# Feed-forward with seven half-block products instead of eight, for 38 of 44 pairs of units

## The chip, the cores and the metric

The kernel runs on one core of a Trainium2 chip. The metric is the device time of one execution in microseconds; lower is better. A core has five engines that run side by side, each with its own list of instructions in a fixed order: TensorE (PE, matrix products; PEld are its weight loads), VectorE (DVE), ScalarE (ACT), GpSimd (POOL) and SyncE (SP, which issues most transfers). They wait for each other through semaphores.

## The reference

Two blocks are computed, one after the other. The change lies in the second one's feed-forward, which stands at the end of each of its two layers (here cut to what matters):

```
D_MODEL = 1024; FF_HIDDEN = 2816; 512 tokens, 256 context tokens
def swiglu(h, w_i, w_o):
    g, u = jnp.split(h @ w_i, 2, axis=-1)
    return (jax.nn.silu(g) * u) @ w_o
...
xl = xl + ml[5] * rms_norm(swiglu(adaln(xl, g[2], ml[3], ml[4]), w_ffn_in[l], w_ffn_out[l]), g[3])
if with_ctx:      # layer 0 only
    xc = xc + mc[5] * rms_norm(swiglu(adaln(xc, g[2], mc[3], mc[4]), w_ffn_in[l], w_ffn_out[l]), g[3])
```

`h @ w_i` has 2 x 2816 columns: 22 blocks of 128 for the gate g and 22 for u. Block m of g and block m of u make a pair of units; there are 22 pairs a layer and 44 in all.

## The kernel before, in words

All products are in float32 split in two: a value is hi + lo, where hi is the value rounded to a shorter form (fp32r) and lo is the rest, and a product is hi·hi + hi·lo + lo·hi, three matmuls. Weights come in by `wsplit` (L272): SP loads 128x1024 float32 values into a buffer `raw` (two buffers), ScalarE makes `hi` (L288), VectorE makes `lo` as raw - hi (L289); `hi` and `lo` have four buffers each. In a unit's raw tile the 1024 columns are 8 blocks of 128x128, one for each 128 of the 1024 inputs. The hidden activations lie transposed, as hTh and hTl (hi and lo), 8 blocks of 128 inputs by 512 tokens, and as hThc and hTlc for the 256 context tokens.

The pairs are worked through in chunks: pairs 0-1, 2-5, 6-9, 10-13, 14-17, then 18-19 and 20-21 in layer 0, 18-21 in layer 1. For each chunk `hidden` (L1672) makes each pair's product with the first weights: for each of its two units, 24 matmuls of 512 columns (`mm_a_g`, L301, L302, L305), in layer 0 also 24 of 256 columns for the context. Then come tanh on ScalarE (L1691), two products on VectorE (L1692, L1693) and the split of the result into `ph` (ScalarE) and `pl` (VectorE), both by `split_into` (L564). After the chunk's pairs, `part` (L1779) multiplies ph and pl by the second weights: for each block of 128 tokens (four in layer 1, six in layer 0) and each half of the 1024 outputs, three matmuls of 512 columns for each pair (`mm_b_g`, L321 to L323), which VectorE adds to `y` (L1791). The first chunk of a layer starts while the tokens are still being normalized, in halves of 256 tokens.

The order on each engine is that of the code, with two exceptions: weights are loaded and split early, by a priority of 3000 steps, as far as buffers allow, and in layer 0 a background (`mod_steps`, L433) of products for the modulation weights runs on VectorE, advanced by `tick`, which counts the columns that PE has been given. SP issues the loads in the order in which they are asked for; a load that waits for its buffer holds up the ones behind it.

Of the kernel before, what the change touches and what calls it, by code (L numbers as in the profile page):

```python
# [251 lines left out]
class Builder:  # L252
# [1418 lines left out]

    def hidden(self, l, ms, segs, fp, NN, bufs, late=None, post=None):  # L1672

        nc, A = self.nc, self.A
# [20 lines left out]
        return ph, pl  # L1695

    def layer2(self, l, hx, vx, hp, hT, hc, vt, fill, src, srcc, stop=None):
# [8 lines left out]
        hy = ExitStack()  # L1706
        hp = self.pool(hy, f"hy{l}")
        with tc.tile_pool(name=f"psf{l}", bufs=2, space=PSUM, reuse_waits="tile") as pp, ExitStack() as c1:
# [48 lines left out]
            ends = [0, 2, 6, 10, 14, 18, 20, 22] if l == 0 else [0, 2, 6, 10, 14, 18, 22]  # L1757
            chunks = [list(range(a, b)) for a, b in zip(ends, ends[1:])]
            ys = {}
            vt = fill = None  # L1760
            for ci, ch in enumerate(chunks):
# [7 lines left out]
                if ci:  # L1769
                    self.hf_act = last  # L1770
                for ms in [ch] if ci == 0 else [[m] for m in ch]:
                    h, lo = self.hidden(l, ms, ctxs + halves if ci == 0 else [(hT, 0, 0, T)] + ctxs, fp, 128 * nt,
                                        2 if last and l == 0 else 6, late if ci == 0 else None, post)
                    ph.update(h)
                    pl.update(lo)
# [17 lines left out]
                if not last:  # L1793
                    for n in range(2):
                        for c in order:
                            part(c, n)
                    if ci == len(chunks) - 2:
                        self.pump(100)
                    continue
                pend = []  # L1800
                for i, c in enumerate(order):
                    v = c // 4
                    ss, d = self.t(self.small, [128, 2], F32, "ss2", 7), []
                    for n in range(2):
                        part(c, n)
                        d.append(self.res_half(rp, ys[c][:, 512 * n:512 * n + 512], G[v], n, ss, n == 0))
# [146 lines left out]
```

## Time and profile before

| | us |
|---|---|
| median of three runs (2586.1 to 2595.94) | 2591.81 |
| the profiled execution | 2587.33 |
| its span in the profile | 2585.5 |
| PE busy in it | 2511.3 |
| VectorE (DVE) busy | 1516.8 |
| ScalarE (ACT) busy | 1031.9 |
| GpSimd (POOL) busy | 241.7 |

The mean granted clock of PE was 0.993 of 2.4 GHz. A row of a timeline gives the start, the duration, the engine, the line of the kernel, the operation with what it writes and reads, and in brackets how long the engine stood idle before it and what ended the wait. A matmul's duration is longer than its share of PE, since matmuls overlap; what one costs is read from the starts.

### The profile page before, as it was taken

How to read it: one execution, taken by the hardware profiler on the slowest of the kernel's cores; microseconds unless marked ns; L12 is line 12 of the kernel's file. 1: busy time of each engine (PE TensorE's matmuls, PEld its weight loads, DVE VectorE, ACT ScalarE, POOL GpSimd, SP SyncE). 2: the span in 40 equal slices, each digit the busy share in tenths (PEclk: the TensorE clock that was granted, in tenths of full speed). 3: DMA queues.
4: the chain of work that ended last, by engine and by line, in shares of the span. 5: the costliest groups of instructions: out<-in, count | busy, mean ns of one | idle time of the engine just before them, and what ended most of it. 6: DMA issues, size and time to landing. Idle time of an engine off the chain costs nothing.

```text
span 2585.5 us, 38643 instructions
## 1 busy us (share of the span) xinstructions
PE 2511.3 (97%) x15587; PEld 2071.2 (80%) x15587; DVE 1516.8 (59%) x2502; ACT 1031.9 (40%) x1962; POOL 241.7 (9%) x288
## 2 busy tenths in 40 slices
PE   8999999999999999999999999999999999999997
PEld 7777887787777888777988888888788777887886
DVE  5657588645365577666756544445567766443434
ACT  6523333333444544465631211212655466522222
POOL 0000012102000000512100000000100412000001
PEclk9999999999999999999999999999999999999999
DMA  5424364342131211522543333332211434322222
GB/s 187 159 73 162 107 228 131 98 131 74 58 130 66 82 34 53 146 81 101 190 146 123 131 122 105 127 120 90 90 58 50 120 110 147 115 91 97 91 97 81
DMA packets 85169, 284.63 MB, mean 110 GB/s; under 512 B 12176, under 2 KB 15072, under 8 KB 84608
## 3 DMA queue, kind: packets, MB, share of 16 engines
q1 hardware_dynamic: 78880, 263.50, 30.0%
q0 software_dynamic: 4864, 15.74, 2.2%
q10 hardware_dynamic: 1248, 2.95, 0.4%
q8 instruction: 122, 2.00, 0.3%
q14 instruction: 55, 0.45, 0.1%
HBM read 253.78 MB, written 21.00 MB: 106 GB/s over the span
## 4 chain that ended last, share of the span: by engine, by line
PE 77%; DVE 7%; issue 5%; ACT 5%; DMA 3%; POOL 2%; SPq 0%; DVEq 0%; POOLq 0%; ACTq 0%
PE acc L301 13%; PE acc L305 13%; PE acc L302 13%; PE acc L321 9%; PE acc L323 9%; PE acc L322 9%; DVE lo L289 2%; ACT hi L288 1%; PE tp L1460 1%; PE at L1431 1%; DMA raw<-in_wo 1%; PE tp L1453 1%; ACT junk L344 1%; ACT hf L388 1%; PE at L650 1%
## 5 line engine op out<-in xcount | busy, mean ns | idle before, releaser
L289 DVE TENSOR_TENSOR lo<-raw,hi 128x1024 fp32r<-128x1024 f32 (+1 forms) x321 | 388.0, 1211 | 400.0 <-ACT hi L288 279.2
L288 ACT ACTIVATE hi<-raw 128x1024 fp32r<-128x1024 f32 (+1 forms) x321 | 335.9, 1048 | 559.2 <-PE acc L323 228.4
L301 PE MATMUL acc<-hTh,hi 128*128 128x512 f32 (+1 forms) x1408 | 547.6, 393 | 5.2 <-ACT hTh L565 2.7
L302 PE MATMUL acc<-hTl,hi 128*128 128x512 f32 (+1 forms) x1408 | 542.2, 389 | 0.3 <-DVE hTl L566 0.2
L305 PE MATMUL acc<-hTh,lo 128*128 128x512 f32 (+1 forms) x1408 | 352.0, 388 | 0.0
L321 PE MATMUL acc<-hi,hTh 128*128 128x512 f32 (+3 forms) x832 | 317.0, 383 | 5.9 <-ACT hi L288 2.4
L301 PEld LDWEIGHTS acc<-hTh,hi 128*128 128x128 f32 x1408 | 266.7, 190 | 65.3 <-issue 3.9
L322 PE MATMUL acc<-lo,hTh 128*128 128x512 f32 (+3 forms) x832 | 310.9, 374 | 2.9 <-DVE lo L289 2.6
L323 PE MATMUL acc<-hi,hTl 128*128 128x512 f32 (+3 forms) x832 | 311.2, 375 | 0.4 <-DVE hTl L566 0.4
L302 PEld LDWEIGHTS acc<-hTl,hi 128*128 128x128 f32 x1408 | 267.4, 190 | 54.7 <-DVE hTl L566 0.7
L305 PEld LDWEIGHTS acc<-hTh,lo 128*128 128x128 f32 x1408 | 254.8, 188 | 55.8 <-issue 0.2
L321 PEld LDWEIGHTS acc<-hi,hTh 128*128 128x128 f32 x832 | 157.1, 189 | 38.4 <-issue 6.6
L322 PEld LDWEIGHTS acc<-lo,hTh 128*128 128x128 f32 x832 | 157.7, 190 | 29.4 <-DVE lo L289 7.1
L323 PEld LDWEIGHTS acc<-hi,hTl 128*128 128x128 f32 x832 | 157.4, 189 | 27.6 <-DVE hTl L566 2.7
L321 PE MATMUL acc<-hi,ph 128*128 128x512 f32 x440 | 175.0, 398 | 0.0
L323 PE MATMUL acc<-hi,pl 128*128 128x512 f32 x440 | 173.8, 396 | 0.0
L322 PE MATMUL acc<-lo,ph 128*128 128x512 f32 x440 | 173.3, 394 | 0.0
L301 PE MATMUL acc<-hThc,hi 128*128 128x256 f32 x608 | 149.2, 283 | 0.0
L302 PE MATMUL acc<-hTlc,hi 128*128 128x256 f32 x608 | 148.0, 281 | 0.0
L433 DVE SCALAR_TENSOR_TENSOR bgraw<-bgraw,cb 128x1024 f32<-128x1024 f32 x96 | 117.1, 1219 | 17.7 <-DMA bgraw<-in_w_mod 16.7
L1791 DVE TENSOR_TENSOR y<-y,acc 128x512 f32<-128x512 f32 x112 | 76.5, 686 | 82.1 <-PE acc L323 81.7
L301 PEld LDWEIGHTS acc<-hThc,hi 128*128 128x128 f32 x608 | 114.4, 188 | 2.5
(340 smaller groups left out, 3697.8 us busy)
## 6 DMA issues: line engine op xcount, KB each, us to landing
bgraw<-in_w_mod SPq DMA_DIRECT2D x96, 512.0 KB, 3.3
raw<-in_wf_in SPq DMA_DIRECT2D x88, 512.0 KB, 3.3
raw<-in_wf_out SPq DMA_DIRECT2D x44, 512.0 KB, 3.3
raw<-in_wb_a SPq DMA_DIRECT2D x38, 512.0 KB, 3.8
raw<-in_wi_a SPq DMA_DIRECT2D x36, 512.0 KB, 3.3
raw<-in_wo SPq DMA_DIRECT2D x32, 512.0 KB, 3.5
xt<-xd SPq DMA_DIRECT2D x16, 512.0 KB, 3.6
raw<-in_wb_v SPq DMA_DIRECT2D x12, 512.0 KB, 3.4
```

Of the source, the lines that this page charges most:

```text
L288: nc.scalar.activation(out=hi[:, :n], in_=raw[:, :n], func=AF.Copy)
L289: self.pin = nc.vector.tensor_tensor(out=lo[:, :n], in0=raw[:, :n], in1=hi[:, :n].bitcast(F32), op=ALU.subtract)
L301: mm(ps, lhsT=wh[:, k], rhs=xh[:, k, n0:n0 + n], start=(k == 0), stop=False)
L302: mm(ps, lhsT=wh[:, k], rhs=xl[:, k, n0:n0 + n], start=False, stop=False)
L305: mm(ps, lhsT=wl[:, k], rhs=xh[:, k, n0:n0 + n], start=False, stop=(k == KT - 1))
L321: mm(ps, lhsT=xh, rhs=wh[:, j], start=(k == 0), stop=False)
L322: mm(ps, lhsT=xh, rhs=wl[:, j], start=False, stop=False)
L323: mm(ps, lhsT=xl, rhs=wh[:, j], start=False, stop=(k == nk - 1))
L344: self.nc.scalar.activation(out=junk[:, :x.shape[-1]], in_=x, func=AF.Square, accum_out=dst)
L388: nc.scalar.activation(out=hf[:, j], in_=ps[:, j], func=AF.Identity, scale=a[:, k:k + 1], bias=b[:, k:k + 1])
L433: nc.vector.scalar_tensor_tensor(out, raw, 1.0, cb[:, v], ALU.mult, ALU.mult, accum_out=md[:, v, k:k + 1])
L1791: nc.vector.tensor_tensor(out=ys[c][:, hs], in0=ys[c][:, hs], in1=ps, op=ALU.add)
```

## The change

A pair's product is seen as a product of two matrices of 2 x 2 blocks: the weights A have the two units as rows and the two halves of the 1024 inputs as columns (A11 and A12 for the gate unit, A21 and A22 for the other), the activations B have the halves of the inputs as rows and the two halves of 256 tokens as columns. The plain product takes eight block products; the changed one takes seven, of sums of blocks:

- with token sums t1 = B12 - B11, t2 = B22 - t1, t3 = B22 - B12 and t4 = B21 - t2 (made once a layer, `token_sums`), and weight sums made for each pair from the raw weights;
- r1 = A11·B11, then + A12·B21 (the gate unit, first half of the tokens);
- r7 = A22·t4, then + (A11 - A21)·t3;
- r5 = (A21 + A22)·t1, then + (A12 - (A21 + A22 - A11))·B22;
- r2 = (A21 + A22 - A11)·t2;
- and the other three results by additions on VectorE, from s1 = A11·B11 + r2, s4 = A22·t4, s5 = (A21 + A22)·t1 - s4, r5 and r7.

Each block product is 12 matmuls of 256 columns (4 blocks of inputs, three matmuls each). The path is taken in both layers from the second chunk on, except in layer 0's last chunk: 18 and 20 pairs. The context's product in layer 0 stays as it was, with A22 and A21 of one unit and A11, A12 of the other. The sums of weights run on GpSimd, in place, on the raw tile; so a pair's raw weights are split four times (w[3], w[0], w[2], w[1]) instead of twice. The raw weights of these pairs go into other buffers: in layer 1 those of the first block's context activations, which are free by then and which the token sums also use as scratch. The first pair of a chunk has its weights prepared during the products with the second weights, and `part` leaves out its last pair's three matmuls until three parts have done the others. The diff, cut to its core:

```diff
+    def token_sums(self, hT, tt, xy):
+        ...
+        op(y, l[0][1], l[0][0], ALU.subtract, nc.gpsimd)
+        op(x, h[0][1], h[0][0], ALU.subtract)
+        op(x, x, y, ALU.add)
+        self.split_into(x, *tt[0])
+        op(y, h[1][1], x, ALU.subtract)
+        op(y, y, l[1][1], ALU.add)
+        self.split_into(y, *tt[1])
+        op(x, h[1][1], h[0][1], ALU.subtract, nc.gpsimd)
+        op(y, h[1][0], y, ALU.subtract)
+        op(y, y, l[1][0], ALU.add)
+        self.split_into(y, *tt[3])
+        op(x, x, l[1][1], ALU.add)
+        op(x, x, l[0][1], ALU.subtract)
+        self.split_into(x, *tt[2])
+
+    def sevens(self, l, hT, tt, hc, fp, rp, NN, raws, fa):
+        ...
+        def weights(m, early=False):
+            ...
+            w = ws[m] = {3: parts(pair(), rb, 512 if hc is None else 1024)}
+            op(a22, a21, a22, ALU.add)
+            op(a21, a11, a21, ALU.subtract)
+            yield
+            w2 = pair()
+            w[0] = parts(pair(), ra)
+            op(a11, a22, a11, ALU.subtract)
+            op(a12, a12, a11, ALU.subtract)
+            yield
+            w[2] = parts(w2, rb)
+            ...
+        def hidden(m, nxt, more):
+            ...
+            r7 = acc()
+            prod(r7, w[3], 1, t4, True)
+            ...
+            act(out=s4, in_=r7, func=AF.Copy)
+            ...
+            r1 = acc()
+            prod(r1, w[0], 0, b11, True)
+            act(out=s1, in_=r1, func=AF.Copy)
+            w[1] = parts(pair(), raw.pop(m)[0])
+            tail()
+            ...
+            r5 = acc()
+            prod(r5, w[2], 1, t1, True)
+            act(out=s5, in_=r5, func=AF.Copy)
+            tt2(s5, s5, s4, ALU.subtract)
+            next(nxt, 0)
+            prod(r7, w[2], 0, t3, False)
+            prod(r1, w[0], 1, b21, False)
+            next(nxt, 0)
+            more()
+            ...
+            gate(a[:, :256], r1)
+            r2 = acc()
+            prod(r2, w[1], 0, t2, True)
+            tt2(s1, s1, r2, ALU.add)
+            tt2(c21, s1, r7, ALU.add)
+            tt2(c22, c21, s5, ALU.add)
+            prod(r5, w[1], 1, b22, False)
+            next(nxt, 0)
+            ...
+                tt2(c12, s1, r5, ALU.add)
+                gate(a[:, 256:], c12)
+                yield from out(a, c2, ph[:, :T], pl[:, :T])
...
+            def raws(m):
+                if l == 0:
+                    pool, tag = ((fp, "raw"), (self.wraw, "raw"))[m % 2]
+                    return [self.t(pool, [128, 1024], F32, tag, 2) for _ in range(2)]
+                t = self.t(hp0, [128, 2, 1024], F32, ("hThc", "hTlc")[m % 2])
+                return t[:, 0], t[:, 1]
...
-                    self.mm_b(ps, lambda k: (ph[ch[k]][:, sl], pl[ch[k]][:, sl]), us[n], len(ch))
+                    g = self.mm_b_g(ps, lambda k: (ph[ch[k]][:, sl], pl[ch[k]][:, sl]), us[n], len(ch))
+                    for _ in range(len(ch) - 1):
+                        next(g)
+
+                    yield
+                    drain(g)
```

VectorE in layer 1, one pair within a chunk, before. The names are those of the code; fa is the gate's buffer, acc a product's result in PSUM, and the numbers tell tiles apart.

```order
L289 TENSOR_TENSOR lo_21542<-raw_21539,hi_21541 128x1024
L1692 SCALAR_TENSOR_TENSOR fa_21438<-fa_21438,acc_21413 128x512
L289 TENSOR_TENSOR lo_21548<-raw_21545,hi_21547 128x1024
L1693 SCALAR_TENSOR_TENSOR fa_21438<-fa_21438,acc_21441 128x512
L566 TENSOR_TENSOR pl_21400<-fa_21438,ph_21399 128x512
```

VectorE in layer 1, one pair within a chunk, now. dy and hf are the buffers of the copies s1, s4, s5 and of the sums; the raw weights lie in hThc and hTlc.

```order
L1737 TENSOR_TENSOR dy_23102<-dy_23102,dy_23101 128x256
L1746 TENSOR_TENSOR lo_23145<-hThc_23050,hi_23144 128x512
L1746 TENSOR_TENSOR lo_23177<-hThc_23050,hi_23176 128x1024
L1787 SCALAR_TENSOR_TENSOR fa_23185<-fa_23185,acc_23109 128x256
L1737 TENSOR_TENSOR dy_23101<-dy_23101,acc_23188 128x256
L1737 TENSOR_TENSOR hf_23103<-dy_23101,acc_23088 128x256
L1737 TENSOR_TENSOR hf_23103<-hf_23103,dy_23102 128x256
L1746 TENSOR_TENSOR lo_23175<-hThc_23050,hi_23174 128x1024
L1737 TENSOR_TENSOR dy_23102<-dy_23101,acc_23129 128x256
L1787 SCALAR_TENSOR_TENSOR fa_23185<-fa_23185,dy_23102 128x256
L1790 SCALAR_TENSOR_TENSOR fa_23185<-fa_23185,hf_23103 128x512
L1746 TENSOR_TENSOR lo_23256<-hThc_23050,hi_23255 128x1024
```

Five rows have become thirteen (the pair's last, the lo of its result, L1737 into pl, comes right behind the last row here): four splits of weights instead of two, and nine operations on results instead of three, four of which read PSUM (acc).

GpSimd at the same place, now; before, it has no row there between the last normalization of the tokens and the end of the layer. The rows are the two token sums of layer 1 and the weight sums of its first six pairs on the new path, four each.

```order
L1705 TENSOR_TENSOR hThc_21511<-hTl_20855 128x1024
L1705 TENSOR_TENSOR hThc_21511<-hTh_20854 128x1024
L1760 TENSOR_TENSOR hThc_21530<-hThc_21530 128x512 x4
L1760 TENSOR_TENSOR hTlc_21629<-hTlc_21629 128x512 x4
L1760 TENSOR_TENSOR hThc_21722<-hThc_21722 128x512 x4
L1760 TENSOR_TENSOR hTlc_21854<-hTlc_21854 128x512 x4
L1760 TENSOR_TENSOR hThc_21986<-hThc_21986 128x512 x4
L1760 TENSOR_TENSOR hTlc_22293<-hTlc_22293 128x512 x4
```

Each of these reads and writes SBUF alone.

VectorE at the start of the new path in layer 1, now: the token sums stand among the last operations of the first chunk (L566 into hTl are the last splits of the normalized tokens, L1692 to L1693 and L566 into pl the first chunk's results).

```order
L1705 TENSOR_TENSOR hThc_21511<-hThc_21511,hTl_20855 128x1024
L566 TENSOR_TENSOR pl_21210<-fa_21422,ph_21209 128x256
L1693 SCALAR_TENSOR_TENSOR fa_21478<-fa_21478,acc_21481 128x256
L566 TENSOR_TENSOR hTl_21510<-hThc_21511,hTh_21509 128x1024
L566 TENSOR_TENSOR pl_21224<-fa_21478,ph_21223 128x256
L1705 TENSOR_TENSOR hThc_21511<-hTh_20854,hThc_21511 128x1024
L1705 TENSOR_TENSOR hThc_21511<-hThc_21511,hTl_20855 128x1024 x2
L566 TENSOR_TENSOR hTl_21510<-hThc_21511,hTh_21509 128x1024 x2
L1746 TENSOR_TENSOR lo_21614<-hThc_21530,hi_21613 128x512
L1746 TENSOR_TENSOR lo_21622<-hThc_21530,hi_21621 128x1024
```

The last two rows are the first split weights of the third pair, whose raw tile (hThc_21530) is the same memory as the scratch of the token sums (hThc_21511).

## Rows read from the trace of the kernel before

**Rows 1.** The page: span, busy time of the engines, the chain.
```profile
span 2585.5 us, 38643 instructions
PE 2511.3 (97%) x15587; PEld 2071.2 (80%) x15587; DVE 1516.8 (59%) x2502; ACT 1031.9 (40%) x1962; POOL 241.7 (9%) x288
PE 77%; DVE 7%; issue 5%; ACT 5%; DMA 3%; POOL 2%; SPq 0%; DVEq 0%; POOLq 0%; ACTq 0%
```

**Rows 2.** Feed-forward stretches: length, PE, PEld, DVE, ACT, POOL busy, clock, DMA, GB/s.
```profile
1312.00:1790.00 478.00, 478.00 (x2498) 405.08 (x2497) 248.16 (x382) 99.53 (x138) 0.00 (x0) 1.00 0.36 120
2230.00:2555.00 325.00, 325.00 (x1388) 260.09 (x1387) 130.16 (x152) 88.23 (x104) 0.33 (x1) 1.00 0.27 91
```

**Rows 3.** Timeline of PE, layer 0: starts of products with 512, then 256 columns.
```profile
1426.95 0.39 PE L301 MATMUL acc<-hTh,hi 128*128 128x512 f32 x1
...
1432.57 0.39 PE L301 MATMUL acc<-hTh,hi 128*128 128x512 f32 x1
...
1438.19 0.28 PE L301 MATMUL acc<-hThc,hi 128*128 128x256 f32 x1
...
1441.01 0.28 PE L301 MATMUL acc<-hThc,hi 128*128 128x256 f32 x1
```

**Rows 4.** Groups by line and shape: busy us, mean ns | idle before.
```profile
L289 DVE TENSOR_TENSOR lo<-raw,hi 128x1024 fp32r<-128x1024 f32 x304 | 372.1, 1226 | 378.5 <-ACT hi L288 274.7 <-PE acc L305 94.0 <-issue 6.3
L433 DVE SCALAR_TENSOR_TENSOR bgraw<-bgraw,cb 128x1024 f32<-128x1024 f32 x96 | 117.1, 1219 | 17.7 <-DMA bgraw<-in_w_mod 16.7
L1791 DVE TENSOR_TENSOR y<-y,acc 128x512 f32<-128x512 f32 x112 | 76.5, 686 | 82.1 <-PE acc L323 81.7
L566 DVE TENSOR_TENSOR pl<-fa,ph 128x512 fp32r<-128x512 f32 x40 | 27.7, 693 | 28.0 <-ACT ph L565 28.0
L1692 DVE SCALAR_TENSOR_TENSOR fa<-fa,acc 128x512 f32<-128x512 f32 x40 | 27.4, 684 | 49.7 <-ACT fa L1691 49.7
L1692 DVE SCALAR_TENSOR_TENSOR fa<-fa,acc 128x256 f32<-128x256 f32 x30 | 12.4, 415 | 0.1
...
L288 ACT ACTIVATE hi<-raw 128x1024 fp32r<-128x1024 f32 x304 | 321.8, 1060 | 533.4 <-PE acc L323 228.2 <-PE acc L302 203.8 <-DMA raw<-in_wf_in 18.7
L565 ACT ACTIVATE ph<-fa 128x512 fp32r<-128x512 f32 x40 | 25.3, 632 | 157.3 <-DVE fa L1693 157.3
L1691 ACT ACTIVATE fa<-acc 128x256 f32<-128x256 f32 x30 | 11.2, 373 | 0.0
...
L1521 POOL TENSOR_TENSOR oh<-oh,gth 128x512 f32<-128x512 f32 x10 | 12.9, 1288 | 54.9 <-DVE gth L1520 54.8
...
L301 PEld LDWEIGHTS acc<-hThc,hi 128*128 128x128 f32 x608 | 114.4, 188 | 2.5
```

**Rows 5.** Timeline, GpSimd beside VectorE at three places: start us, us, instruction.
```profile
1218.01 2.54 POOL L1655 TENSOR_TENSOR vt<-vt,G 128x512 f32<-128x512 f32 x2
...
1219.58 2.06 DVE L289 TENSOR_TENSOR lo<-raw,hi 128x1024 fp32r<-128x1024 f32 x1 [2.08 <-ACT hi L288]
...
2168.99 1.23 DVE L289 TENSOR_TENSOR lo<-raw,hi 128x1024 fp32r<-128x1024 f32 x1 [0.54 <-ACT hi L288]
2169.64 1.72 POOL L1655 TENSOR_TENSOR vt<-vt,G 128x512 f32<-128x512 f32 x1 [0.61 <-ACT junk L344]
...
2554.67 1.30 POOL L1655 TENSOR_TENSOR y<-y,G 128x512 f32<-128x512 f32 x1 [348.27 <-ACT junk L344]
2555.02 0.69 DVE L1791 TENSOR_TENSOR y<-y,acc 128x512 f32<-128x512 f32 x1 [0.24 <-PE acc L323]
```

**Rows 6.** The page's DMA issues: count, KB each, us from issue to landing.
```profile
raw<-in_wf_in SPq DMA_DIRECT2D x88, 512.0 KB, 3.3
```

**Rows 7.** Stretches at the start of layer 1's feed-forward, columns as in rows 2.
```profile
2190.00:2196.00 6.00, 1.60 (x11) 0.99 (x9) 4.65 (x9) 5.95 (x14) 0.00 (x0) 1.00 0.72 249
2196.00:2200.00 4.00, 3.88 (x18) 3.69 (x19) 2.37 (x4) 3.81 (x9) 0.54 (x1) 0.57 0.44 137
2200.00:2204.00 4.00, 4.00 (x36) 4.00 (x35) 3.13 (x6) 2.11 (x6) 0.54 (x1) 1.00 0.65 227
```

More of the change, by code (lines that the diff above doesn't have):

```diff
@@ L1670, in norm_vecs, with hidden @@
         return a[:, v], b[:, v]
-    def hidden(self, l, ms, segs, fp, NN, bufs, late=None, post=None):
+    def hidden(self, l, ms, segs, fp, NN, bufs, fa, late=None, post=None):
         nc, A = self.nc, self.A
@@ L1695, in hidden, with op @@
         return ph, pl
+    def token_sums(self, hT, tt, xy):
+        nc = self.nc
+        h, l = [[[x[:, 4 * k:4 * k + 4, 256 * t:256 * t + 256].bitcast(F32) for t in range(2)] for k in range(2)] for x in hT]
+        x, y = xy
+        def op(o, a, b, op, e=nc.vector):
+            e.tensor_tensor(out=o, in0=a, in1=b, op=op)
+        op(y, l[0][1], l[0][0], ALU.subtract, nc.gpsimd)
[12 more added lines that the diff above has]
+        self.split_into(x, *tt[2])
@@ L1706, in layer2 @@
         hy = ExitStack()
-        hp = self.pool(hy, f"hy{l}")
+        hp0, hp = hp, self.pool(hy, f"hy{l}")
         with tc.tile_pool(name=f"psf{l}", bufs=2, space=PSUM, reuse_waits="tile") as pp, ExitStack() as c1:
@@ L1758, in layer2 @@
             chunks = [list(range(a, b)) for a, b in zip(ends, ends[1:])]
+            end7 = ends[-2] if l == 0 else ends[-1]
             ys = {}
@@ L1770, in layer2 @@
                     self.hf_act = last
[L1771 to L1775, printed above, removed]
+                seven = ci > 0 and not (last and l == 0)
+                if seven:
+                    for m in ch:
+                        ph[m], pl[m] = s7[2](m, s7[1](m + 1) if m + 1 in ch else iter(()),
+                                             lambda: s7[0](m + 2) if m + 1 in ch and m + 2 < end7 else None)
+                    s7[3]()
+                else:
+                    for ms in [ch] if ci == 0 else [[m] for m in ch]:
+                        h, lo = self.hidden(l, ms, ctxs + halves if ci == 0 else [(hT, 0, 0, T)] + ctxs, fp, 128 * nt,
+                                            2 if last and l == 0 else 4, 3 if last and l == 0 else fa, late if ci == 0 else None, post)
+                        ph.update(h)
+                        pl.update(lo)
+                if ci == 0:
+                    tt = sums()
+                    self.token_sums(hT, tt, [x.rearrange("p (k n) -> p k n", n=256) for x in raws(0)])
+                    s7 = self.sevens(l, hT, tt, hc, fp, rp, 128 * nt, raws, fa)
+                    s7[0](ch[-1] + 1)
                 us = [None, None]
@@ L1794, in layer2 @@
                     for n in range(2):
-                        for c in order:
-                            part(c, n)
+                        gs = [part(c, n) for c in order]
+                        for i in range(0, nt, 3):
+                            for _ in range(2):
+                                for g in gs[i:i + 3]:
+                                    next(g, 0)
+                    if ch[-1] + 1 < end7:
+                        with tc.high_priority(offset=3000):
+                            drain(s7[1](ch[-1] + 1, True))
+                        s7[0](ch[-1] + 2)
                     if ci == len(chunks) - 2:
@@ L1804, in layer2 @@
                     for n in range(2):
-                        part(c, n)
+                        drain(part(c, n))
                         d.append(self.res_half(rp, ys[c][:, 512 * n:512 * n + 512], G[v], n, ss, n == 0))
```

84 lines of the change are left out of this document (83 added, 1 removed).

## The prediction

> **What bounds the kernel now.** I read the page's busy shares and chain first. PE is busy 97% of a span of 2585.5 us, the chain lies on PE for 77% of it, and VectorE, at 59%, is the only other engine above 40% [rows 1]. Then the stretches: in most of layer 0's feed-forward (1312 to 1790 us) and of layer 1's (2230 to 2555 us) PE has no gap at all, its granted clock is 1.00, which is the 2.4 GHz level, and GpSimd does nothing [rows 2]. So an us of PE taken out there is an us of time, as long as the others keep up. VectorE is busy 52% of the first stretch and 40% of the second, with background products of the modulation weights in the first.
>
> **The gross saving.** In layer 0 a unit's product for the 512 tokens starts at 1426.95 and the next at 1432.57: 24 matmuls in 5.62 us, 0.234 each; 24 matmuls of 256 columns (the context's) take 2.82 us, 0.1175 each [rows 3]. So two matmuls of 256 columns cost one of 512 almost exactly. A pair was 48 x 0.234 = 11.24 us; the seven products are 7 x 12 = 84 matmuls of 256 columns, 84 x 0.1175 = 9.87 us. That is 1.37 us a pair and 52.1 us for 38 pairs (24.7 in layer 0, 27.4 in layer 1) if no one is late.
>
> A rule of the Trainium skill speaks against this term: by "TensorE: Matmul & The Clock Gate", section "Back-to-back issue gap", the spacing in a stream of weight loads and matmuls is set by both, about 81 ns at 128 columns and 131 ns at 512. A straight line between the two gives an estimate of 98 ns at 256, so 84 x 0.098 = 8.2 us against 48 x 0.131 = 6.3, and the seven would be 1.9 us a pair slower. The two spacings of [rows 3] disagree with it, and they decide.
>
> **What is added beside it, layer 1.** By the program's order a pair now has on VectorE four subtractions for lo (one of them half size, since without context only half of the fourth weight block is needed), seven 256-column operations, one product of 512 and the lo of the result; on GpSimd four sums of 128x512 of the raw weights, where it had none; on ScalarE four hi, three copies, two tanh and one ph. Nearest rows [rows 4]: lo 128x1024 1.226 us, VectorE 128x256 0.415, 128x512 0.684 and 0.693, GpSimd 128x512 1.288, ScalarE hi 1.060, 128x256 0.373, 128x512 0.632. VectorE: 3 x 1.226 + 0.693 + 7 x 0.415 + 0.684 + 0.693 = 8.65 us; ScalarE: under 3.9 + 5 x 0.373 + 0.632 = 6.4; GpSimd: 4 x 1.288 = 5.15. Each by itself is below 9.87, and the gain would stand.
>
> But they aren't by themselves. While GpSimd's L1655 runs from 1218.01 to 1220.55, the lo started at 1219.58 takes 2.06 us [rows 5]: against its mean of 1.226 it lost 0.83 us, and most of its work came after GpSimd's end. At 2169.64 it is the other way about: a lo is running and GpSimd's operation takes 1.72 instead of 1.29. A VectorE add of which one input is in PSUM (2555.02) starts inside a GpSimd operation and still takes 0.69. So operations with both inputs in SBUF and GpSimd's run one after the other. The Trainium skill says the same more sharply ("SBUF — State Buffer", section "Who interferes with whom"): the second read port is one exclusive lock, held for the whole instruction, and a VectorE instruction with two SBUF inputs contends. By it the engines' times add; without it the larger alone would count. The rows agree with the lock.
>
> Of the 8.65 us, four 256-column operations read PSUM; the rest, 6.99 us, is locked: 6.99 + 5.15 = 12.14 us a pair, more than the 9.87 of the products and more than the old 11.24. The lower bound of the pace is thus 9.87 (the lock seldom meets), the upper 12.14 for a pair whose preparation falls within the pair before. I take nearly the upper one, because both the rows and the written order set GpSimd's sums right beside the lo's. The first pair of a chunk has its weights prepared during the products with the second weights (8 x 12 x 0.234 = 22.5 us, in which VectorE has little to do): 9.9 us. The second starts with a little lead: 11.0. The third and fourth are paced: 12.1 each. Sum 45.1 against 4 x 11.24 = 44.96, and about 0.3 for the tail of a chunk. PE's waits will stand at the fifth and seventh products (the second weight block's hi and lo behind GpSimd's sums). Five chunks: -2 us in all, where 27.4 were gained gross. Layer 1's whole gain goes.
>
> **Layer 0.** Here a pair has the context's 48 matmuls as well, 5.64 us, so 15.5 us of PE. The fourth weight block is whole (+0.53) and the context's result adds a lo of 0.415 under the lock (and two operations from PSUM): 13.1 us, below 15.5. The gain stands in most pairs. What stands against it is the background (L433, two SBUF inputs, 1.219 us). In chunks 2-5 and 6-9 one pair each has four of them: 13.1 + 4 x 1.22 = 18.0, -2.5 us each. Behind chunk 2-5 the order sets 15 of them, 12 y adds (L1791's 0.686), four lo, three early lo and GpSimd's four sums into products of 12 x 12 x 0.234 = 33.7 us: 18.3 + 8.2 + 4.9 + 3.7 + 5.15 = 40.3, up to -6.6; I take -5, since the y adds read PSUM and go beside GpSimd. Tails -2.5. Layer 0: 24.7 - 5 - 5 - 2.5 = +12 us (bounds: +24.7, and +5).
>
> **The two entries.** The token sums are new work between the first chunk and the first seven-product pair: eight VectorE sums and four lo of 128x1024 (12 x 1.226 = 14.7 us), four hi, and two GpSimd sums of that size, which no row shows: 1.29 to 2.6 us (one or two of 128x512), I take 2.5. In layer 1 a VectorE sum stands ahead of the last hTl, behind GpSimd's first sum: PE waits some 2.7 us for hTl. The raw weights of the third pair (index 2) go into the buffer that the token sums use as scratch, so that their load starts only after the last lo. Landing takes 3.3 us [rows 6], hi of half size 0.6 and lo 0.69: 4.6 us behind the last token sum, which ends about when PE has run out of the first chunk's products (96 x 0.1175 + 48 x 0.234 = 22.5 us, against 14.7 + 2.5 + some 5 us of other VectorE work). Then GpSimd's two sums, hi and lo, 4.9 us, must be in before the fifth product, with 2.8 us of products ahead: another 2. And idling costs twice: after the waits at 2190 to 2196 the clock was at 0.57 for 4 us, 18 matmuls where the next 4 us hold 36 [rows 7], so 1.7 us go after such a stop. 2.7 + 4.6 + 2 + 1.7, less what overlaps: -10 in layer 1 (bounds -5, -13). In layer 0 the scratch is the same, but 768 tokens give half as much cover again: -4 (-1, -7). The last chunk of layer 1 drains its parts one by one, so that the last pair's tail (0.415 + 0.373 + 0.415 + 0.684 + 0.632 + 0.693 = 3.2 us) has 9 x 0.234 = 2.1 us of cover: -1.5 with what follows.
>
> The raw loads are as many as before and land within a pair's time. The loads of the second weights stand behind them on SP's queue and are asked for a chunk ahead: nothing.
>
> **Sum**, against the profiled execution: +12 - 4 - 2 - 10 - 1.5 = -5.5. Its time was 2587.3 (span 2585.5), so 2592.8; the median of the runs shown is 4.5 above it, and on that scale I say 2597.
>
> **Rivals.**
> *The saving comes through (16%).* GpSimd's sums fall beside the waits of VectorE and the lock costs little; both layers keep 1.37 a pair and only entries and ends count: 52.1 - 14 - 1.5 = 36.6, 2555. For it: VectorE idles half the time in rows 2. Against it: 12.14 against 9.87, in three pairs of four.
> *Half of it (17%).* Layer 0 keeps all its 24.7, since the context's products cover the lock and the background moves aside, layer 1 is neutral, and the entries cost 4 instead of 14: 24.7 - 2 - 4 - 1.5 = 17, 2575.
> *Slower (23%).* One mechanism: PE's waits in layer 1's paced pairs are each over 2 us (12.1 - 9.9), a good part of the 4.4 us (of 6) that PE stood idle before the clock fell [rows 7]. If every paced pair pays the 1.7 us of half clock, 15 x 1.7 = 25.5 us come on top: 2623. It decides if the waits come in one piece; split between the fifth and the seventh product, they may be too short.
> *Weight loads bind (2%).* A weight load lasts 0.19 us, longer than 0.1175; if the new stream couldn't hide it, 84 x 0.188 = 15.8 us a pair, 4.6 more, 2760 or so. The context's matmuls of [rows 3] have the same loads and don't show it.
>
> **Numbers.** The forecast itself has 42%, with its own range of 2583 to 2610. A measurement of this kernel tells 0.5%, 13 us, from no change: 2579 to 2605. Faster: 16 + 12 of the half case + 4 of the forecast's lower edge = 32%. Slower: 23 + 2 + 4 of its upper edge = 29%. Same: 39%. The range goes to 2553, leaving out half of the first rival, and up to 2627, leaving out the last and a third of the slower case.
>
> **What would show it.** Right: in layer 1 PE's waits at the new products name VectorE's lo and ScalarE's hi of the second weight block, VectorE's lo means well over 1.23 us, GpSimd's sums over 1.29, chunks of about 45 us; in layer 0 the pairs without background take 15.5 us, without waits; PE stands still for 8 to 11 us at layer 1's first seven-product pair. Wrong: PE has no gap in 2230 to 2555 (first rival), or its granted clock falls in every pair there (third), or 84 matmuls take other than 9.9 us.

## The result: slower by 0.7%

The changed kernel takes 2611.23 us (median of four runs, 2608.51 to 2614.53), the kernel before 2593.88 beside it. The ratio is 1.0072, with a 95% interval of 1.0045 to 1.0098. The forecast was 2597, with a range up to 2627 and its weight on "no change": the time lies in the range, just above the forecast's own part of it (2583 to 2610) and nearer to the rival called slower.

### The profile page after: what moved, and what is told of

It reads as the page before. It is cut to its first block, busy times and chain, and to the rows that moved or that the text cites. A ratio compares the mean times of both kernels' runs of the same rounds, so it can differ in the third digit from the quotient of the medians.

```text
span 2608.6 us, 42234 instructions
## 1 busy us (share of the span) xinstructions
PE 2490.1 (95%) x16955; PEld 2115.7 (81%) x16955; DVE 1738.5 (67%) x2830; ACT 1136.7 (44%) x2198; POOL 513.1 (20%) x444
## 5 line engine op out<-in xcount | busy, mean ns | idle before, releaser
L289 DVE TENSOR_TENSOR lo<-raw,hi 128x1024 fp32r<-128x1024 f32 (+2 forms) x245 | 295.0, 1207 | 231.4 <-ACT hi L288 176.6
L288 ACT ACTIVATE hi<-raw 128x1024 fp32r<-128x1024 f32 (+2 forms) x245 | 255.1, 1043 | 282.7 <-PE acc L302 113.9
L301 PE MATMUL acc<-hTh,hi 128*128 128x512 f32 (+1 forms) x800 | 307.1, 391 | 5.2 <-ACT hTh L565 2.7
L302 PE MATMUL acc<-hTl,hi 128*128 128x512 f32 (+1 forms) x800 | 301.4, 383 | 2.7 <-DVE hTl L566 2.6
L1776 PE MATMUL acc<-hTh,hi 128*128 128x256 f32 x776 | 195.9, 285 | 12.6 <-ACT hi L1736 6.4
L305 PE MATMUL acc<-hTh,lo 128*128 128x512 f32 (+1 forms) x800 | 197.3, 381 | 0.0
L1777 PE MATMUL acc<-hTl,hi 128*128 128x256 f32 x776 | 192.8, 281 | 0.0
L301 PEld LDWEIGHTS acc<-hTh,hi 128*128 128x128 f32 x800 | 153.0, 192 | 37.0 <-issue 3.2
L302 PEld LDWEIGHTS acc<-hTl,hi 128*128 128x128 f32 x800 | 153.1, 192 | 30.0 <-DVE hTl L566 3.5
L305 PEld LDWEIGHTS acc<-hTh,lo 128*128 128x128 f32 x800 | 140.1, 188 | 27.8 <-issue 0.2
L1776 PEld LDWEIGHTS acc<-hTh,hi 128*128 128x128 f32 x776 | 146.7, 189 | 18.4 <-ACT hi L1736 8.6
```

The source lines that it names most:

```text
L288: nc.scalar.activation(out=hi[:, :n], in_=raw[:, :n], func=AF.Copy)
L289: self.pin = nc.vector.tensor_tensor(out=lo[:, :n], in0=raw[:, :n], in1=hi[:, :n].bitcast(F32), op=ALU.subtract)
L301: mm(ps, lhsT=wh[:, k], rhs=xh[:, k, n0:n0 + n], start=(k == 0), stop=False)
L302: mm(ps, lhsT=wh[:, k], rhs=xl[:, k, n0:n0 + n], start=False, stop=False)
L305: mm(ps, lhsT=wl[:, k], rhs=xh[:, k, n0:n0 + n], start=False, stop=(k == KT - 1))
L1776: mm(ps, lhsT=wh[:, 4 * o + k], rhs=xh[:, k], start=(first and k == 0), stop=False, skip_group_check=True)
```

## The profile after

The page, as [rows 1]: PE is busy 21 us less in a span 23 us longer; VectorE has 222 us more, GpSimd twice its time.

```profile
span 2608.6 us, 42234 instructions
PE 2490.1 (95%) x16955; PEld 2115.7 (81%) x16955; DVE 1738.5 (67%) x2830; ACT 1136.7 (44%) x2198; POOL 513.1 (20%) x444
```

Four stretches, columns as in [rows 2]: layer 0's chunk 2-5, its chunk 10-13, layer 1's chunk 2-5 and its chunk 6-9, the matmuls of the first weights each time.

```profile
1318.00:1391.00 73.00, 66.90 (x529) 65.81 (x530) 62.12 (x90) 29.15 (x51) 30.48 (x16) 0.95 0.34 117
1531.00:1594.50 63.50, 62.88 (x532) 62.62 (x531) 47.67 (x69) 26.70 (x47) 19.39 (x12) 1.00 0.32 110
2256.00:2304.00 48.00, 44.05 (x338) 41.78 (x339) 33.46 (x48) 23.22 (x40) 28.25 (x16) 0.96 0.23 84
2327.00:2369.00 42.00, 40.81 (x334) 39.66 (x334) 31.18 (x46) 21.10 (x37) 21.33 (x12) 1.00 0.26 92
```

Where PE had no gap it now has some, and in the first chunk of each layer on the new path the clock falls too. Cut into stages by the starts on PE's timeline (first and second: the products with the first and second weights; us), the two traces stand so:

| stage | before | after | difference |
|---|---|---|---|
| up to layer 0's feed-forward | 1254.4 | 1258.6 | +4.2 |
| layer 0: chunk 0-1, first + second | 37.5 + 16.8 | 40.6 + 19.7 | +6.0 |
| layer 0: first of 2-5, 6-9, 10-13, 14-17, 18-19 | 67.8, 67.6, 67.8, 67.6, 33.8 | 72.2, 67.9, 63.3, 65.9, 31.3 | -4.0 |
| layer 0: their second | 33.6 x4, 16.9 | 35.0, 37.3, 34.7, 33.8, 18.7 | +8.2 |
| layer 0's feed-forward as a whole, last chunk included | 572.4 | 581.0 | +8.6 |
| between the feed-forwards | 369.2 | 372.3 | +3.1 |
| layer 1: chunk 0-1, first + second | 26.9 + 11.2 | 29.0 + 15.8 | +6.7 |
| layer 1: first of the five chunks | 45.0 x5 | 47.1, 42.5, 42.4, 42.5, 42.5 | -8.0 |
| layer 1: second of the first four | 22.5 x4 | 23.0, 23.6, 24.3, 24.8 | +5.6 |
| layer 1: the last second products and the end | 36.4 | 39.3 | +2.9 |
| layer 1's feed-forward to the end | 389.5 | 396.7 | +7.2 |

The traces differ by 23 us, the medians by 17: the execution profiled before (2587.33) is 6.5 us below the median of its runs, the one after (2610.77) 0.5 us. So some 6 us of the differences here are spread from run to run.

What PE waited for in layer 0's new pairs (1312 to 1780 us): us in total, times, the longest.

```profile
PE acc L1776 <- DVE fa L1787: 10.5, 9, 2.2
PE acc L1776 <- ACT hi L1736: 2.7, 1, 2.7
PE acc L321 <- ACT ph L1736: 2.4, 2, 1.9
PE acc L301 <- DVE fa L1790: 2.2, 4, 0.6
PE acc L323 <- DVE pl L1737: 1.2, 2, 0.9
```

The first row is new to the forecast: the first matmul of a pair (L1776) waits for the gate of the context's product (L1787) of the pair before, which still holds the PSUM buffer that it needs. Why the gate is late stands in the timelines of GpSimd and VectorE at 1326 to 1338 us (start, duration):

```profile
1325.97 2.16 POOL L1760 TENSOR_TENSOR raw<-raw 128x512 f32<-128x512 f32 x1
```

```profile
1326.90 2.32 DVE L433 SCALAR_TENSOR_TENSOR bgraw<-bgraw,cb 128x1024 f32<-128x1024 f32 x1
...
1329.26 1.22 DVE L1746 TENSOR_TENSOR lo<-raw,hi 128x1024 fp32r<-128x1024 f32 x1
1332.84 1.23 DVE L433 SCALAR_TENSOR_TENSOR bgjunk<-bgraw,cb 128x1024 bf16<-128x1024 f32 x1 [2.36 <-DMA bgraw<-in_w_mod]
...
1334.11 1.22 DVE L433 SCALAR_TENSOR_TENSOR bgraw<-bgraw,cb 128x1024 f32<-128x1024 f32 x1
...
1335.60 2.35 DVE L1746 TENSOR_TENSOR lo<-raw,hi 128x1024 fp32r<-128x1024 f32 x2
1337.87 0.41 DVE L1787 SCALAR_TENSOR_TENSOR fa<-fa,acc 128x256 f32<-128x256 f32 x1
```

A background product takes 2.32 us beside GpSimd's sum instead of the 1.22 of [rows 4]. In chunk 2-5 it is no exception: the mean of the group is 1744 ns there (over all of layer 0's new pairs 1382 ns, 51 of them).

```profile
L433 DVE SCALAR_TENSOR_TENSOR bgraw<-bgraw,cb 128x1024 f32<-128x1024 f32 x7 | 12.2, 1744 | 0.0
```

Another waits 2.36 us for its transfer, and all behind it on VectorE waits as well; the gate comes at 1337.87. On PE:

```profile
1338.34 0.38 PE L1776 MATMUL acc<-xn,hi 128*128 128x256 f32 x1 [2.24 <-DVE fa L1787]
...
1340.05 0.41 PE L302 MATMUL acc<-hTlc,hi 128*128 128x256 f32 x1
1340.26 0.41 PE L301 MATMUL acc<-hThc,hi 128*128 128x256 f32 x1
```

From 1.5 us after this stop of 2.24 us the matmuls start 0.21 us apart, at 1.2 GHz, where 0.12 is the rule. The granted clock averaged 0.61 over 4.4 us, much as after the waits of [rows 7]; that is 0.39 x 4.4 = 1.7 us on top of the 2.24:

```profile
1339.80:1344.20 4.40, 4.40 (x26) 4.36 (x25) 4.40 (x7) 1.33 (x2) 4.24 (x3) 0.61 0.01 4
1344.20:1352.00 7.80, 7.80 (x68) 7.78 (x67) 7.80 (x17) 3.30 (x7) 0.77 (x1) 1.00 0.49 171
```

It doesn't follow every time. In an experiment below (e4) PE stops for 2.21 us at the same place, and the granted clock stays at 1.00 behind it:

```profile
1338.98 0.38 PE L1776 MATMUL acc<-xn,hi 128*128 128x256 f32 x1 [2.21 <-DVE fa L1787]
1339.00:1347.00 8.00, 6.58 (x54) 6.38 (x55) 7.99 (x15) 1.75 (x3) 6.39 (x4) 1.00 0.19 60
```

## Experiments

The median of each stands with the ratio to the kernel before, run beside it, and the 95% interval of the ratio. The experiments are called e1 to e12; stages are cut as in the table above.

**The layers apart.** The path is taken in one layer only; the other is as before.

```diff
-                seven = ci > 0 and not (last and l == 0)
+                seven = l == 1 and ci > 0 and not (last and l == 0)    # e2: l == 0
```

> The seven products in layer 1's 20 pairs alone; layer 0 as before. Theory (each layer pays by itself what its two traces differ by): layer 1's feed-forward to the end took 389.5 us before and 396.7 after, so about 7 us slower than the kernel before, some 2600. Rival (the forecast's split: layer 1 pays 12 to 14 us, layer 0 gains 8): 2605 to 2608. It would be wrong for both if this kernel were not slower than before.

> The seven products in layer 0's 18 pairs alone; layer 1 as before. Theory: the two traces put 8.6 us of loss into layer 0's feed-forward, so some 2602; the 7 us that lie before and between the feed-forwards are chance and not in it. Rival (the forecast: layer 0 gains 12 less 4 at its entry): 2585. Second rival (the 7 us outside belong to the change): 2609.

Measured: layer 1 alone (e1) 2597.55 us, ratio 1.0013 (1.0004 to 1.0023); layer 0 alone (e2) 2591.97, 0.9997 (0.9987 to 1.0006). Each is close to no change, layer 0 alone far from the 2602 expected of it. Their sum, +0.1%, isn't the +0.7% of both. In the traces layer 0's feed-forward takes 576.1 us when it is alone and 581.0 with layer 1 changed too, though the order of instructions is the same on every engine up to layer 1; what differs is how the waits fall (chunk 14-17 62.7 us against 65.9). With layer 1 it is the other way about, 401.1 alone and 396.7 with layer 0 changed. So the feed-forwards do add up: 3.7 + 11.6 = 15.3 us more than before when each is alone, 8.6 + 7.2 = 15.8 together. What doesn't add up lies outside them; I come back to this below.

**Whether GpSimd's sums are the cause.** First they are left out; then, in layer 1 alone, they are made into a buffer that no one reads.

```diff
-            op = lambda o, x, y, op: pin(nc.gpsimd.tensor_tensor(out=o, in0=x, in1=y, op=op))
+            op = lambda o, x, y, op: None                                                                        # e3
+            op = lambda o, x, y, op: pin(nc.gpsimd.tensor_tensor(out=idle, in0=x, in1=y, op=op)) if l else None  # e5
```

> The changed kernel without the four sums of weights of each pair on GpSimd (left out: the products are then of unsummed weights). Everything else, matmuls, splits, copies, gates, stays. Theory (GpSimd and VectorE's operations with two SBUF inputs run one after the other, and that fills VectorE's time): layer 1's chunks fall from 42.4 to about 39.7 us, the waits at the start of the second products vanish, in layer 0 the waits for the context's gate shrink; 5 x 4 + 12 to 15 = some 33 us less, about 2578. Rival (the chain of copies, gates and splits of VectorE and ScalarE in the written order is late by itself): less than 10 us less, above 2601.

> As e3_no_weight_sums (no weight sums feed the products in either layer), but in layer 1 GpSimd still makes four sums of 128x512 a pair from the raw weights, into a buffer that no one reads, so that nothing waits for them. Theory (the lock: what costs is that VectorE and GpSimd take turns): layer 1's chunks stay at 41 to 42.4 us instead of e3's 39.9, its second products stay late, and the whole is 7 to 15 us above e3's 2569, 2576 to 2584. Rival (latency: what costs is that hi and lo of the second weight block wait for GpSimd's result): as e3, 2569 to 2572.

Without the sums (e3): 2569.13 us, 0.9909 (0.9893 to 0.9924), 42 us below the changed kernel, more than the 33 expected. Layer 1's chunks are 39.9 us (the first 41.1) and layer 0's 62.2 to 64.8. But of the 52 us of gross saving only 24 are kept, and no weight sum has a part in what is still lost: against the kernel before, the chunks 0-1 are 5.4 and 6.6 us longer, the second products 6.6 and 2.8, the end of layer 1 2.4.

With sums that nothing waits for (e5): 2613.49, 1.0072 (1.0043 to 1.0101), all 44 us back and far more than the 7 to 15 expected; in the traces 41 of them lie in layer 1's feed-forward. The loads aren't later for GpSimd's reads: in layer 1's new chunks ScalarE waits for a load of the first weights once in either run, for 2.4 us. So that VectorE and GpSimd take turns is enough to lose this much, with nothing waiting for a sum. The splits of weights in layer 1's feed-forward (busy us, mean ns), without sums:

```profile
L1746 DVE TENSOR_TENSOR lo<-hTlc,hi 128x1024 fp32r<-128x1024 f32 x30 | 36.7, 1222 | 11.9 <-ACT hi L1736 11.9
```

in the changed kernel, with GpSimd's sums beside them:

```profile
L1746 DVE TENSOR_TENSOR lo<-hThc,hi 128x1024 fp32r<-128x1024 f32 x30 | 38.7, 1290 | 36.8 <-ACT hi L1736 36.8
...
L1760 POOL TENSOR_TENSOR hTlc<-hTlc 128x512 f32<-128x512 f32 x40 | 71.0, 1776 | 71.0 <-DVE lo L1746 68.6
L1760 POOL TENSOR_TENSOR hThc<-hThc 128x512 f32<-128x512 f32 x40 | 66.7, 1667 | 114.7 <-DVE lo L1746 112.3
```

and with sums that no one reads:

```profile
L1749 DVE TENSOR_TENSOR lo<-hTlc,hi 128x1024 fp32r<-128x1024 f32 x30 | 48.0, 1601 | 1.4 <-ACT hi L1739 1.4
...
L1740 DVE TENSOR_TENSOR pl<-fa,ph 128x512 fp32r<-128x512 f32 x19 | 22.7, 1195 | 0.0
```

In the changed kernel it is mostly GpSimd that yields (1.67 to 1.78 us for 1.29). With sums that no one reads GpSimd's take 1.61 to 1.68, and VectorE yields as well (1.52 to 1.60 for 1.22); what PE waits for then is lo in the chunks (10.2 us) and the last pair's ph and pl at the second products (14.0 us). In one of these, stops of 4.5 us in all and a clock of 0.89 made 30.5 us of 22.5:

```profile
2354.00:2384.50 30.50, 25.98 (x100) 19.83 (x99) 16.18 (x24) 5.69 (x7) 6.27 (x4) 0.89 0.28 96
```

e5 is thus a bound and not the changed kernel's own share: there, 2.5 us a chunk of layer 1 lie between 39.9 and 42.4. How they come about in the changed kernel is read from a steady pair of chunk 6-9:

```profile
2344.65 7.38 POOL L1760 TENSOR_TENSOR hThc<-hThc 128x512 f32<-128x512 f32 x4 [4.00 <-DVE lo L1746]
2348.46 1.06 ACT L1736 ACTIVATE hi<-hThc 128x1024 fp32r<-128x1024 f32 x1 [4.08 <-POOL hThc L1760]
2349.56 1.33 DVE L1746 TENSOR_TENSOR lo<-hThc,hi 128x1024 fp32r<-128x1024 f32 x1 [2.27 <-ACT hi L1736]
2350.94 0.74 PE L1779 MATMUL acc<-hTh,lo 128*128 128x256 f32 x4 [0.15 <-DVE lo L1746]
2352.00 0.38 PE L1776 MATMUL acc<-hTh,hi 128*128 128x256 f32 x1 [0.31 <-ACT dy L1736]
```

Here a pair does wait for the sums' results. ScalarE stands idle for 4.08 us until two sums are made, VectorE for 2.27 until hi is, and PE waits for lo and then for a copy that stands behind that hi on ScalarE. The turns make the wait longer, since the four sums take 7.38 us instead of 4 x 1.29 = 5.15. No run tells apart how much of the 2.5 us is the chain itself and how much the turns.

**What makes layer 0 late.** The background products over an eighth of their columns; the context's gate moved ahead of them; and two of four weight sums given to VectorE.

```diff
+                        few = 128 if bufs == 1 else 1024                                          # e9
-                        nc.vector.scalar_tensor_tensor(out, raw, 1.0, cb[:, v], ALU.mult, ALU.mult,
+                        nc.vector.scalar_tensor_tensor(out[:, :few], raw[:, :few], 1.0, cb[:, v, :few], ALU.mult, ALU.mult,
...
             prod(r5, w[2], 1, t1, True)                                                           # e6
+            if ctx:
+                a0 = self.t(fp, [128, 512], F32, "fa", fa)[:, :CT]
+                gate(a0, ctx[0])
...
-            op(a22, a21, a22, ALU.add)                                                            # e8
+            tt2(a22, a21, a22, ALU.add)
-            op(a11, a22, a11, ALU.subtract)
+            tt2(a11, a22, a11, ALU.subtract)
-            act(out=s5, in_=r5, func=AF.Copy)
-            tt2(s5, s5, s4, ALU.subtract)
+            tt2(s5, r5, s4, ALU.subtract)
```

> The changed kernel with layer 0's background products (L433) over 128 of the 1024 columns, so that each takes little of VectorE and of the lock (left out: seven eighths of those sums; loads, waits and places stay). Theory (in layer 0 the background products, slowed by GpSimd's sums from 1.22 to 1.74 us, push back the context's gate for which PE waits): layer 0's feed-forward falls from 581 us to 562 to 568, the whole to about 2595. Rival (the lock between GpSimd's sums and the splits alone makes layer 0 late, as in layer 1): under 5 us less.

> The changed kernel with the gate of the context's product (tanh and L1787's product, layer 0 only) ahead of VectorE's s5, splits and background products, right behind the fifth product, instead of behind the two that follow it. Theory (in layer 0 PE waits 10.5 us for that gate, which holds the PSUM buffer of the next pair's first product, and loses about as much to the half clock behind the longer waits): 10 to 15 us less, about 2599. Rival (VectorE and GpSimd are simply full there, so the wait moves to the next operation, the context's result or the split): under 4 us less.

> The changed kernel with two of the four weight sums of a pair on VectorE instead of GpSimd, and s5 subtracted straight from PSUM (one copy of ScalarE less, one VectorE operation out of the lock). By the lock a pair's time on VectorE and GpSimd together falls from 12.1 to 6.99 - 0.42 + 2 x 0.69 + 2 x 1.29 = 10.5 us, while VectorE's own goes from 8.65 to 10.0. Theory (the lock): layer 1's chunks fall from 42.4 to about 40.5, seconds by 1, layer 0 alike: 15 to 22 us less, some 2592. Rival (VectorE's own work is what counts, not the lock): slower than 2611.

With a small background (e9): 2593.37 us, 0.9997 (0.9985 to 1.0010), 18 us less than the changed kernel; layer 0's feed-forward takes 563.9 us for 581.0. The list of waits for its new pairs has 1.4 us at the gate, where there were 10.5:

```profile
PE acc L321 <- ACT ph L1737: 2.3, 1, 2.3
PE acc L1777 <- DVE fa L1788: 1.4, 1, 1.4
```

So in layer 0 it takes both, the background and GpSimd's sums: without either the gate behind them in VectorE's order is in time (in e3 it isn't on the list at all). That background products wait for transfers isn't what it takes: VectorE has 45 us of such waits in e3 and 78 in e9, where the gate is in time, and 47 in the changed kernel. The second products of layer 0 stay late without the sums (6.6 us in e3) and with a small background (6.2), so neither is what makes them late.

Moving the gate alone (e6) missed: 2616.45, 1.0083 (1.0064 to 1.0102). PE still waits 9.7 us there, in fewer and longer stops, and 5.8 us instead of 2.4 for ph; the place of that one instruction isn't what makes it late.

```profile
PE acc L1776 <- DVE fa L1787: 9.7, 5, 3.0
```

Giving VectorE two sums (e8) was worse, 2623.12, 1.0111 (1.0089 to 1.0132), as its rival had said. Layer 1's chunks rose to 43.4 (41.9, and a product of 1.5 that moved behind the first ones with the second weights), layer 0's to 78.8, 71.6, 65.2 and 68.5. In layer 0 PE waits 19.4 us for the gate, and VectorE 13.5 us, in its own order, for GpSimd's other sums (18.9 us in layer 1):

```profile
PE acc L1776 <- DVE fa L1787: 19.4, 8, 4.5
DVE raw L1737 <- POOL raw L1760: 13.5, 13, 1.2
```

The sum by the lock (12.1 down to 10.5) leaves such waits out. Whether they or the 10.0 us of VectorE's own work made it slower isn't told apart.

**Entry and tails of layer 1.**

```diff
-                    self.token_sums(hT, tt, [x.rearrange("p (k n) -> p k n", n=256) for x in raws(0)])
+                    self.token_sums(hT, tt, [x.rearrange("p (k n) -> p k n", n=256) for x in raws(l)])     # e4
...
-                        for i in range(0, nt, 3):
+                        step = 4 if ci and l == 1 else 3                                                 # e7
+                        for i in range(0, nt, step):
```

> The token sums of layer 1 use the other pair's buffer as scratch (that of the fourth pair), so that the load of the third pair's weights needs not wait for them. Theory (that load is what PE waits for at layer 1's first new pair): the waits of 3.7 and of some 2 us there go, with the half clock behind them: 4 to 8 us less, about 2605. Rival (the token sums and splits themselves are what is late): the wait only changes its name, 2611. Layer 0 is as in the changed kernel.

> The changed kernel with four parts instead of three that do all pairs but the last before the first of them needs it, in layer 1's chunks. Theory (PE's waits for ph and pl at the start of the second products, 0.5 to 2.3 us a chunk and the end's 3, are for lack of cover: a fourth part adds 9 matmuls, 2.1 us): 4 to 6 us less, about 2606. Rival (the fourth part needs a PSUM buffer that the last pair still holds, so PE waits there instead): no change.

The other scratch (e4): 2610.80, 1.0067 (1.0050 to 1.0083). The entry got 2.2 us shorter (14.6 + 46.1 for 15.8 + 47.1), which the whole doesn't show; the wait is for more than the load.

Four parts (e7): 2602.17, 1.0039 (1.0025 to 1.0053), 9 us less, more than expected. In the traces layer 1's feed-forward is 6.3 us shorter, which is what the theory had; the rest lies ahead of layer 0's feed-forward (1254.8 us for 1258.6), which the edit doesn't touch. Layer 1's second products are back at 22.4 us in the first four chunks, so their 0.5 to 2.3 us were lack of cover for the last pair's ph. Two stops in the changed kernel that are gone:

```profile
2509.66 0.50 PE L321 MATMUL acc<-hi,ph 128*128 128x512 f32 x1 [1.28 <-ACT ph L1736]
2511.01 0.51 PE L323 MATMUL acc<-hi,pl 128*128 128x512 f32 x1 [0.61 <-DVE pl L1737]
```

**A version that keeps some of it.** The new path only where the reasons above leave room: in layer 1 from pair 6 (e10), in layer 0 from pair 10 too (e11), the token sums written in the chunk before, four parts, s5 from PSUM; and in e12 two buffers for the gate in layer 0's first chunks, where the change had left one of three.

```diff
+            first7 = (99, 2)[l]                                         # e11, e12: (3, 2)
...
-                seven = ci > 0 and not (last and l == 0)
+                seven = ci >= first7 and not (last and l == 0)
+                if ci == first7 - 1:
+                    tt = sums()
...
+                            a = self.t(fp, [128, 4, 256], F32R, "T1", 2)[:, :2].rearrange("p a b -> p (a b)").bitcast(F32)[:, :n]   # e12
```

> Layer 1 alone, 16 pairs, from pair 6 on: the token sums stand in the chunk before, behind the entry of the layer; four parts ahead of the last pair, in the last chunk the first two parts together, and s5 subtracted from PSUM. Layer 0 as before. Theory (entry 10 us, second products 5 to 9 us and the end 3 us were what ate the gain of 2.5 us a chunk): 4 chunks x 2.6 = 10 us gained, less 1 to 3: 0.3% faster than before, about 2584. Rival (the token sums cost as much in their new place): 2592.

> As e10, and in layer 0 the 10 pairs from pair 10 on, where few background products are left; token sums in the chunk before. Theory: layer 0 gains 4.5 + 4.5 + 2.5 us in its three chunks less 3 us at the second products and 1 to 3 for the token sums: 5 to 7 us below e10, some 2578. Rival (layer 0's gains go in waits for the context's gate, and the transfers land later with both layers changed): at or above e10.

> As e11, with two buffers instead of one for the gate's result in layer 0's first two chunks (those of the token sums, still unused then). Theory (the change had cut that buffer from three to one in layer 0 to make room, and that, not the token sums, is why e11's first chunk takes 40.3 + 19.1 us instead of 37.5 + 16.8): 4 to 5 us below e11, about 2579.5, 0.5% faster than before. Rival (the first chunk is late for the order of loads or the fewer buffers of ph): as e11, 2584.

e10: 2590.27, 0.9992 (0.9982 to 1.0002), not told apart from before and near its rival's 2592. A new chunk with its second products takes 66.0 us for 67.5, a gain of 1.5 instead of 2.6 (42.4 us for the pairs, and second products one us late again), and layer 1's chunk 0-1 still takes 28.8 + 12.8 us for 26.9 + 11.2. For the token sums run where they did, some 15.6 us behind the layer's first matmul, wherever the code has them: they are a third exception to the order of the code. GpSimd's first one in the changed kernel and in e10, and PE's stop behind it in e10, for an hTl that VectorE makes after its own first token sum:

```profile
2227.59 2.40 POOL L1705 TENSOR_TENSOR hThc<-hTl 128x1024 f32<-128x1024 f32 x1 [5.24 <-DVE hTl L566]
```

```profile
2216.13 2.40 POOL L1705 TENSOR_TENSOR hThc<-hTl 128x1024 f32<-128x1024 f32 x1 [5.23 <-DVE hTl L566]
2220.27 0.38 PE L302 MATMUL acc<-hTl,hi 128*128 128x256 f32 x1 [1.72 <-DVE hTl L566]
```

So this run doesn't test what the token sums cost in another place. e11: 2584.00, 0.9967 (0.9957 to 0.9977), 6 us below e10, as expected; layer 0's three chunks take 62.3, 63.4 and 31.0, their second products 33.6, 33.6 and 19.0. e12: 2582.67, 0.9954 (0.9942 to 0.9967), 11 us below the kernel before and not told apart from e11. It shortened layer 0's chunk 0-1 by 2.9 us (39.7 + 16.8 for 40.3 + 19.1), not by the 4 to 5 expected. Three of the token sums also run later there (from 1384 us on), so what the single buffer cost isn't told apart from them; of the 2.2 us that stay in the first products, 1.9 are a stop for an hTl behind a token sum of 3.36 us.

## Why the prediction was right, and where not

*The gross saving: right.* Against the spacing of [rows 3] a new pair was put at 9.87 us in layer 1 and 15.5 in layer 0. It takes 9.96 and 15.49 when no one is late; PE in layer 1, the starts of three pairs:

```profile
2326.71 0.28 PE L1776 MATMUL acc<-hTh,hi 128*128 128x256 f32 x1
...
2336.68 0.28 PE L1776 MATMUL acc<-hTh,hi 128*128 128x256 f32 x1
...
2346.64 0.28 PE L1776 MATMUL acc<-hTh,hi 128*128 128x256 f32 x1
```

So the rival of the weight loads falls.

*That the sums beside the splits eat the gain: right*, by e3 and e5. Its size in layer 1 was too high: I put a chunk's pairs at 9.9, 11.0, 12.1 and 12.1 us, 45.1 in all; they took 9.97, 9.97, 11.1 and 11.4, 42.4 in all, since GpSimd's sums in part fall beside operations that read PSUM and the lead of a chunk's first pair lasts longer. And the pace isn't the two engines' times added up: in the steady pair VectorE stands idle for 2.27 us in one wait. PE does wait for hi and lo of the second weight block, as told, but the sign of splits well over 1.23 us was wrong (1.27 to 1.29): GpSimd stretched instead.

*Layer 0: the step that failed.* The sum had a gain of 12 for its pairs and a loss of 4 for the entry; in the trace it loses 4 and 6 (the feed-forward as a whole is 8.6 us longer). I counted VectorE's and GpSimd's time per pair against PE's (13.1 to 18.0 against 15.5) and took what fits as free. But the background runs at 1.74 us instead of 1.22 beside the sums (mean in chunk 2-5), and behind it stands a gate that holds a PSUM buffer, for which PE waits 10.5 us; and the stop at 1336 us was paid again in half clock (1.7 us). e9 puts 18 us on the background's part in this. Of the entry's 6 us, 2.7 are the stop for the first new pair's hi, as told; the rest falls in the first products, where token sums and the gate's single buffer aren't told apart.

*The entry of layer 1: right in size*, 6.7 us in the first chunk and 4.6 in the next against a steady one, for 10 forecast. Its parts weren't all as told: e4 took the load out of the way and saved 2 us of it. PE did stop there, but for 4.7 us and not for the 8 to 11 that were to be seen (ahead of them it waits 1.7 us for hTl, where 2.7 were told):

```profile
2256.69 0.38 PE L1776 MATMUL acc<-hTh,hi 128*128 128x256 f32 x1 [3.75 <-ACT hi L1736]
...
2262.08 0.39 PE L1776 MATMUL acc<-hTh,hi 128*128 128x256 f32 x1 [0.99 <-ACT hi L1736]
```

*Tails: mis-sized.* 2.5 us in layer 0 and 1.5 at the end were forecast, with 0.3 a chunk in layer 1; the second products took 8.2 us more in layer 0 and 5.6 in layer 1, the end 2.9. I reckoned their cover with VectorE free, and it was behind: in layer 1 more cover cures it (e7), in layer 0's first chunks no run tests it.

*The slower rival* came near the result from the wrong place: the half clock does come after stops (2.24, 2.71 and 3.75 us), but in layer 0 and at the entries; layer 1's steady pairs had waits of 1.1 us a chunk, none over 0.3, and a clock of 1.00. Its price was too high by its own premise, too: two pairs of four were paced at 12.1, so ten and not fifteen would pay, 17 us, and 2614.

*That the time fell into the range is in part luck.* Layer 0's feed-forward was to gain 8 us and lost 8.6, layer 1's was to lose 13.5 and lost 7.2, and 7.3 us of the traces' difference lie where the forecast had nothing.

*What stays open.* 7.3 us of the 23 between the two traces lie outside the feed-forwards, where up to layer 1 the instructions are in the same order as in e2, which has 1 us of it. That the execution profiled before lies 6.5 us below its median can make up some 6. In the trace of the changed kernel the clock also falls twice ahead of the first feed-forward where it doesn't in e2 (columns as in [rows 2]; the changed kernel, then e2):

```profile
1047.00:1060.00 13.00, 10.23 (x42) 7.78 (x41) 5.44 (x13) 4.00 (x11) 2.28 (x5) 0.87 0.54 144
1160.00:1175.00 15.00, 12.53 (x77) 9.88 (x76) 13.15 (x26) 10.61 (x24) 0.00 (x0) 0.89 0.31 106
```

```profile
1047.00:1060.00 13.00, 10.60 (x58) 8.43 (x57) 7.35 (x17) 4.00 (x11) 3.76 (x8) 1.00 0.57 147
1160.00:1175.00 15.00, 12.81 (x80) 9.08 (x80) 13.16 (x26) 11.33 (x29) 0.00 (x0) 1.00 0.24 76
```

Some weights land later there, too (one 128x1024 load of the mixer 5.9 us after its issue, 4.4 in e2). In e7 and e8, which change both layers as well, the first feed-forward starts at 1254.8 and 1255.1 us, as before, so part of it is chance. In the medians both layers together cost 17 us and one alone 5 or none. The mean granted clock was 0.989 with both changed, 0.991 and 0.992 with one, and 0.992 before; 0.003 of 2600 us is some 8 us (an estimate), so much of that gap can be clock. Why it is lower with both isn't explained.

## What to carry to other kernels

Fewer matmuls on a busy PE are worth what the other engines leave of them: count what the saved time demands of them in the same stretch, add VectorE's operations on two SBUF inputs to GpSimd's, and then look in the written order for what holds a PSUM buffer behind them, and for the chain from one engine's result through the others to PE. A mean load that fits isn't enough where a single stop can cost more than its length (2.24 us and 1.7 in clock here). After moving an operation in the code, look in the trace whether it moved. Use such a change where there is slack (here from the chunk where the background has thinned) and leave it out elsewhere.

## What the runs showed of the hardware

80 sums on GpSimd that no one reads cost 44 us (e5 against e3). After a single stop of 2.24 us within a full stream PE's granted clock averaged 0.61 over 4.4 us, from some 1.5 us after the restart; after one of 2.21 us at the same place in another run (e4) it stayed at 1.00. Two kernels with the same instructions up to 1250 us can stand 4 to 5 us apart there, in these traces from half clock at different places and from weights that land later.
